# A hybrid attention layer on one core: rope tables in fewer VectorE operations, and a written order from opening to attention

## The chip, the cores and the metric

The kernel runs on one core of one Trainium2 chip. The metric is the device time of one execution in microseconds (us); 0.5% of it is about 5 us. The profile counts from the span's first instruction. PE is TensorE, DVE VectorE, ACT ScalarE, POOL GpSimd, SP the engine whose queue issues nearly all DMAs.

## The reference

One decoder layer over 1024 tokens of width 1024, in float32. The input is normed and modulated (h), one wide projection of h gives the inputs of two attention branches and their gates, each branch is projected back, and the two are merged, projected and added to the input:

```python
h = rmsnorm(x, norm_gain) * (1.0 + scale) + shift
(sb_q, sb_k, sb_v, sb_z, c_q, c_kv, k_rot, mla_z, g_a, g_b) = split(h @ w_in)
o_a = stick_breaking_attention(sb_q, sb_k, sb_v)     # 8 heads of 64
y_a = (o_a * silu(sb_z)) @ w_branch_a
# latent attention: q and k carry 32 rotary columns, rope(x, positions)
y_b = (o_b * silu(mla_z)) @ w_branch_b
x = x + gate * ((sigmoid(g_a) * y_a + sigmoid(g_b) * y_b) @ w_out)
```

`rope` turns 16 pairs of columns by the angles positions * inv_freq. The kernel keeps cos and sin of 1024 tokens x 16 frequencies as two tables of 128 partitions x 128 numbers, which are first used long after, in the latent stage.

## The kernel before

**Split products.** Every operand of a matmul is kept as a rounded part and a remainder (hh and hl, whi and wlo, q0a and so on): a copy into the rounded type (L88 on DVE, L86 on ACT), then a subtraction (`rest`, L96, on DVE or POOL). A product is three matmuls: hi*hi, hi*lo, lo*hi.

**The opening (L419 to L685)** builds hh and hl, eight slices k of h^T, each for two halves q of the tokens, and with them V (four PSUM tiles of tokens) and Q and K of the first head pair (two tiles): `product` L543 adds slice k into six tiles accu[q][0..5] with the PSUM tags g, g, s, s, s, o. The last slice of the second half (L683) goes tile by tile in the order 5, 4, 0, 1, 2, 3, so that ps_o is whole first. For slice k, PE transposes x (L527), ACT writes hh and a full-precision ht (L535), DVE subtracts them into hl (L539, by L96). In the second half the table generator `rope_tables` (L139) is drawn nine yields at a time (L681) between these splits, all on DVE. Its tile rp lies in the buffers of the modulation weights.

**pin_engines (L407)** chains all that was traced since a given point to the previous instruction of the same engine, without semaphores: it fixes each engine's order as written. It is called once, at L685, at the end of the opening. Everything else is ordered by a planner at build time, by its own costs and by when it takes operands to be ready; it also deals out the buffers of a tag. `issue_after(ins)` orders what a block traces on the engine of ins behind ins.

**The change to attention.** Behind L685 stand `evac_q` and `evac_k` (L335, L348) of the first pair: the first half of Q and K was copied to qk0 during the opening, the second lies in accu[1][4] and accu[1][5]. Each half needs 4 ACT copies, 4 DVE remainders and 4 DVE casts, for heads 0 and 1. `store_v` (L565) empties accu[1][0..3]: per tile an ACT copy, a DVE remainder and a DMA to DRAM on SP; `load_v` (L364) reads V of a head pair back. Here the planner chose all orders.

**Jobs (L276).** 30 jobs each project h through 128 columns of w_in: `prep` loads 512 KB of weights on SP (`load_split` L269, into a tile raw of two buffers, a tag shared with qk0), splits them by a cast on DVE (whi) and a subtraction (wlo) on the engine `le`: POOL by default, DVE for job 0. `units` runs 24 matmuls (L299) for each half of the tokens into a PSUM tile by the job's tags; job 0 has tags t and o, most others g and g. `run_jobs` (L304) preps a job between the halves of the one before. The generator is the filler of the attention of head pairs, `sb_pair` (L764), a unit about every second step. A step makes scores on PE (L753), two sigmoids on ACT, a scan on DVE (L757) and a product on POOL (L761); its weights are transposed (L706) and multiplied with V (L723) one step later. Behind L809 jobs 0 and 1 are begun and V of pair 0 is loaded; `gate_sum` (L818) is drawn every fourth step.

Of the kernel before, what the change touches and what calls it, by code (L numbers as in the profile page):

```python
# [19 lines left out]
P = 128  # L20
# [28 lines left out]
def hybrid_layer(ctx: ExitStack, tc: tile.TileContext, x, c, positions, w_ada, b_ada, norm_gain, w_in,  # L49
# [86 lines left out]
    cos_t = base.tile([P, NT, 16], F32, name="cos_t")  # L136
    sin_t = base.tile([P, NT, 16], F32, name="sin_t")

    def rope_tables(pool):  # L139
        eng = nc.vector  # L140
        n = [0]
        slots = pool.tile([P, 32, P], F32, name="rp", tag="wa", bufs=3)

        def new(keep):
            if keep is not None:
                return slots[:, keep]
            n[0] += 1
            return slots[:, n[0] % 26]

        def ts(i, s1, op0, s2=None, op1=None, keep=None):  # L150
            o = new(keep)
            eng.tensor_scalar(out=o, in0=i, scalar1=s1, scalar2=s2, op0=op0, **({"op1": op1} if op1 else {}))
            return o

        def tt(a, b, op, keep=None):
            o = new(keep)
            eng.tensor_tensor(out=o, in0=a, in1=b, op=op)
            return o

        def near(i, unit):  # L160
            m = 1.5 * 2.0 ** 23 * unit
            r = ts(i, m, ALU.add)
            return ts(r, m, ALU.subtract)

        import numpy as np
        inv = np.float32(ROPE_BASE) ** (-np.arange(0, DR, 2, dtype=np.float32) / np.float32(DR))
        ang = new(None)
        av = ang.rearrange("p (t f) -> p t f", f=16)
        for f in range(16):
            eng.tensor_scalar(out=av[:, :, f], in0=pos_c, scalar1=float(inv[f]), scalar2=None,  # L170
                              op0=ALU.mult)
            if f % 4 == 3:
                yield
        from fractions import Fraction
        pi = Fraction(31415926535897932384626433832795028841971693993751, 10 ** 49)
        total = None
        left = ang
        for e in (20, 9, -2, None):
            if e is None:
                part, k, scale = left, Fraction(1) / (2 * pi), 1.0  # L180
            else:
                part = near(left, 2.0 ** e)
                left = tt(left, part, ALU.subtract)
                scale = 2.0 ** -e
                k = Fraction(2) ** e / (2 * pi)
            k -= round(k)
            unit = Fraction(1, 2 ** 12)
            k1 = round(k / unit) * unit
            unit = Fraction(1, 2 ** 24)
            k2 = round((k - k1) / unit) * unit  # L190
            k3 = k - k1 - k2
            whole = ts(part, scale, ALU.mult) if scale != 1.0 else part
            if e is None:
                fr = ts(whole, float(k), ALU.mult)
                total = tt(total, fr, ALU.add)
                break
            t1 = ts(whole, float(k1), ALU.mult)
            yield
            t1 = tt(t1, near(t1, 1.0), ALU.subtract)
            yield  # L200
            t2 = ts(whole, float(k2), ALU.mult)
            yield
            t3 = ts(whole, float(k3), ALU.mult)
            yield
            s = tt(t1, t2, ALU.add)
            yield
            s = tt(s, t3, ALU.add)
            yield
            total = s if total is None else tt(total, s, ALU.add)
            yield  # L210
        turn = tt(total, near(total, 1.0), ALU.subtract)
        yield
        q = ts(near(turn, 0.25), 4.0, ALU.mult, keep=26)
        th = ts(tt(turn, near(turn, 0.25), ALU.subtract), 2.0 * math.pi, ALU.mult, keep=27)
        yield
        t2 = tt(th, th, ALU.mult, keep=28)
        yield

        def poly(cs):
            r = ts(t2, cs[0], ALU.mult, cs[1], ALU.add)  # L220
            for cc in cs[2:]:
                r = ts(tt(r, t2, ALU.mult), cc, ALU.add)
            return r

        fact = math.factorial
        sn = tt(poly([-1.0 / fact(11), 1.0 / fact(9), -1.0 / fact(7), 1.0 / fact(5), -1.0 / fact(3)]), t2, ALU.mult)
        yield
        sn = tt(tt(sn, th, ALU.mult), th, ALU.add, keep=29)
        yield
        cs = tt(poly([1.0 / fact(12), -1.0 / fact(10), 1.0 / fact(8), -1.0 / fact(6), 1.0 / fact(4), -0.5]), t2,  # L230
                ALU.mult)
        cs = ts(cs, 1.0, ALU.add)
        q2 = tt(q, q, ALU.mult)
        yield
        odd = ts(q2, 1.0, ALU.is_equal)
        yield
        m1 = tt(odd, q, ALU.mult)
        yield
        m0 = tt(ts(odd, -1.0, ALU.mult, 1.0, ALU.add), ts(q2, -0.5, ALU.mult, 1.0, ALU.add), ALU.mult)
        yield  # L240
        cv, sv = cos_t.rearrange("p t f -> p (t f)"), sin_t.rearrange("p t f -> p (t f)")
        eng.tensor_tensor(out=cv, in0=tt(m0, cs, ALU.mult), in1=tt(m1, sn, ALU.mult), op=ALU.subtract)
        eng.tensor_tensor(out=sv, in0=tt(m0, sn, ALU.mult), in1=tt(m1, cs, ALU.mult), op=ALU.add)

    def newton(r, v, n):
# [58 lines left out]
    def run_jobs(jobs):  # L304
        for i, j in enumerate(jobs):
            j.prep()
            if i + 1 < len(jobs):
                g = j.units()
                next(g)
                jobs[i + 1].prep()  # L310
                yield
                for _ in g:
                    yield
            else:
                yield from j.units()
# [19 lines left out]
    def evac_q(m):  # L335
        st = pairs[m]

        def f(hf, ps):
            if hf == 0:
                st.q = [qk(f"q{m}a"), qk(f"q{m}b")]  # L340
            s = hsl(hf)
            for h in range(2):
                r0, r1 = (slice(0, 64), slice(64, 128)) if h == 0 else (slice(64, 128), slice(0, 64))
                copy("a", st.q[h][r0, s], ps[r0])
                rest("v", st.q[h][r1, s], ps[r0], st.q[h][r0, s])
        return f

    def evac_k(m):  # L348
        st = pairs[m]

        def f(hf, ps):
            if hf == 0:
                st.k = [qk(f"k{m}a"), qk(f"k{m}b")]
                st.kl = [qk(f"kl{m}a"), qk(f"kl{m}b")]
            s = hsl(hf)
            for h in range(2):
                r0, r1 = (slice(0, 64), slice(64, 128)) if h == 0 else (slice(64, 128), slice(0, 64))
                copy("a", st.k[h][r0, s], ps[r0])
                rest("v", st.kl[h][r0, s], ps[r0], st.k[h][r0, s])
                copy("v", st.k[h][r1, s], rd(st.k[h][r0, s]))  # L360
                copy("v", st.kl[h][r1, s], rd(st.kl[h][r0, s]))
        return f

    def load_v(m):  # L364
        st = pairs[m]
        st.v = sbp.tile([P, NT, 2, P], F32R, name=f"v{m}", tag="v", bufs=2)
        nc.sync.dma_start(out=rd(st.v), in_=v_d[:, :, m])
# [48 lines left out]
    def last_on(name):  # L416
        return last_of[dict(SP=nc.sync, DVE=nc.vector, ACT=nc.scalar, PE=nc.tensor)[name].engine]

    with tc.tile_pool(name="start", bufs=1, **RW, side="right") as st:  # L419
# [145 lines left out]
        def store_v(q, t, pool=st, tag="wa", bufs=3):  # L565
            if pool is st and t % 2 == 0:
                vos[0] = st.tile([P, 2, NPAIR, 2, P], F32R, name="vo", tag="wa", bufs=3)
            vo = vos[0][:, t % 2] if pool is st else pool.tile([P, NPAIR, 2, P], F32R, name="vo", tag=tag, bufs=bufs)
            split_v(vo, accu[q][t], "a")
            nc.sync.dma_start(out=v_d[:, 4 * q + t], in_=rd(vo))  # L570
# [117 lines left out]
    evp = evx.enter_context(tc.tile_pool(name="evp", bufs=2, **RW, side="right"))  # L688
    sbx = ExitStack()
    sbp = sbx.enter_context(tc.tile_pool(name="sbp", bufs=1, **RW, side="right"))  # L690
    for hf in range(2):
        evac_q(0)(hf, qk0[:, 0] if hf == 0 else accu[1][4])
        evac_k(0)(hf, qk0[:, 1] if hf == 0 else accu[1][5])
    for t in range(4):
        store_v(1, t, sbp, "wt", WT_BUFS[0])


    anchor = [None]
    QE = "v"
# [103 lines left out]
    for j, tg in zip(jobs[::-1], "gg,to".split(',')):  # L803
        j.tags = tg
    jobs[0].tags = "to"
    filler = run_jobs(jobs)
    if 1:
        tc.keep_in_program_order(nc.scalar.activation(warm, ones_c, AF.Sigmoid))
    with tc.issue_after(last_on("SP")), tc.issue_after(last_on("DVE")):  # L809
        advance(filler, 1)  # L810
    advance(filler, 1)
    load_v(0)
    ones_r = base.tile([P, 1], F32R, name="ones_r")
    nc.vector.tensor_copy(out=ones_r, in_=ones_c)

# [2 lines left out]
    def gate_sum():  # L818
# [4 lines left out]
            nc.sync.dma_start(out=wgs[k], in_=wada[:, k, 2 * D:3 * D])  # L823

        nc.gpsimd.memset(gsum, 0.0)
        nc.sync.dma_start(out=gsum[0:1], in_=b_ada[:, 2 * D:3 * D])
        load_g(0)
        load_g(1)
        yield
        for k in range(KD):  # L830
            cc = col[:, R_C + k:R_C + k + 1]
# [586 lines left out]
```

## Time and profile before

| | us |
|---|---|
| median of 3 runs | 984.95 (981.52 to 985.64) |
| the profiled execution's own time | 984.33 |
| its span, first to last instruction | 982.5 |
| PE busy | 953.9 (97%) |
| DVE busy | 641.5 (65%) |
| ACT busy | 440.3 (45%) |
| POOL busy | 289.8 (29%) |

Busy shares of PE come from pipelined matmuls, whose ends are modelled: consecutive matmuls overlap in the rows, and the pace is the distance of their starts. In a timeline's row the first number is the start, the second how long the row's instructions lasted together, and the bracket the engine's idle time before them with what ended it. Rows may merge several instructions (x2, x3).

### The profile page before, as it was taken

The numbers are of one execution on the slowest core, as the hardware profiler recorded it, in microseconds if no ns is written. First come the engines' busy times: TensorE is split into PE (matmuls) and PEld (weight loads), VectorE is DVE, ScalarE is ACT, GpSimd is POOL, SyncE is SP. The second block draws the span as 40 slices with busy tenths as digits, with TensorE's granted clock in tenths as the row PEclk, the third lists the DMA queues.
The fourth block names the chain that finished last, engine by engine and source line by source line (L and its number), as shares of the span: only waits on it lengthen the run. The fifth ranks groups of instructions, "written<-read, shape, count | busy, mean of one in ns | idle before, by whom it ended". The sixth has DMA issues, their size and how long they took to land.

```text
span 982.5 us, 14349 instructions
## 1 busy us (share of the span) xinstructions
PE 953.9 (97%) x5132; PEld 824.2 (84%) x5132; DVE 641.5 (65%) x1319; ACT 440.3 (45%) x991; POOL 289.8 (29%) x256
## 2 busy tenths in 40 slices
PE   5999699999999999999999999999999999999997
PEld 4888588888888888888888999988899998878886
DVE  5657756568655966385654454864689997595654
ACT  5453324344524443444443432543488886342211
POOL 1010235344544444354453000621103441101222
PEclk9899899999999999999999999999999999999999
DMA  9911273223331141103212500579554332792232
GB/s 311 332 53 56 87 238 95 73 64 90 129 105 46 54 139 54 54 22 97 76 65 86 150 1 1 192 274 303 180 134 135 104 97 69 248 374 95 83 118 98
DMA packets 112712, 122.39 MB, mean 125 GB/s; under 512 B 14928, under 2 KB 81597, under 8 KB 112256
## 3 DMA queue, kind: packets, MB, share of 16 engines
q1 hardware_dynamic: 112550, 121.44, 39.3%
q8 instruction: 41, 0.67, 0.3%
q14 instruction: 31, 0.25, 0.1%
q10 hardware_dynamic: 90, 0.02, 0.0%
HBM read 86.80 MB, written 34.64 MB: 124 GB/s over the span
## 4 chain that ended last, share of the span: by engine, by line
PE 92%; DVE 4%; DMA 2%; issue 1%; ACT 0%; DVEq 0%; SPq 0%
PE ps_g L299 38%; PE ps_o L723 7%; PE ps_t L706 7%; PE ps_g L935 3%; PE ps_s L1354 3%; PE ps_g L1354 3%; PE ps_t L1354 3%; PE ps_s L936 3%; PE ps_s L1170 2%; PE ps_s L1172 2%; PE ps_s L551 2%; PE ps_s L1171 2%; PE ps_g L551 2%; PE ps_s L754 2%; PE ps_s L753 2%; PE ps_t L1050 2%
## 5 line engine op out<-in xcount | busy, mean ns | idle before, releaser
L299 PE MATMUL ps_g<-hh,whi 128*128 128x512 f32 x448 | 178.8, 399 | 5.4 <-DVE vo L96 5.4
L299 PE MATMUL ps_g<-hl,whi 128*128 128x512 f32 x448 | 177.7, 397 | 0.0
L299 PE MATMUL ps_g<-hh,wlo 128*128 128x512 f32 x448 | 176.8, 395 | 0.0
L757 DVE TENSOR_TENSOR_SCAN surv<-surv,diag 128x128 f32<-128x128 f32 (+3 forms) x64 | 112.6, 1764 | 41.6 <-ACT surv L755 40.8
L96 POOL TENSOR_TENSOR wlo<-raw,whi 128x1024 fp32r<-128x1024 f32 (+1 forms) x37 | 80.8, 2184 | 174.5 <-DVE whi L88 98.2
L96 DVE TENSOR_TENSOR wtl<-ps_t,wth 128x512 fp32r<-128x512 f32 (+1 forms) x192 | 101.6, 548 | 17.6 <-ACT wth L86 16.6
L761 POOL TENSOR_TENSOR beta<-beta,surv 128x127 f32<-128x127 f32 (+3 forms) x64 | 85.4, 1334 | 62.2 <-DVE surv L757 61.6
L299 PEld LDWEIGHTS ps_g<-hh,whi 128*128 128x128 f32 x448 | 85.0, 190 | 21.6 <-DVE vo L96 5.8
L86 ACT ACTIVATE wth<-ps_t 128x512 fp32r<-128x512 f32 (+1 forms) x192 | 90.0, 490 | 23.7 <-PE ps_t L706 21.0
L299 PEld LDWEIGHTS ps_g<-hh,wlo 128*128 128x128 f32 x448 | 84.9, 189 | 17.1
L299 PEld LDWEIGHTS ps_g<-hl,whi 128*128 128x128 f32 x448 | 85.0, 190 | 15.3
L391 ACT ACTIVATE ev<-ps_g 128x512 f32<-128x512 f32 x32 | 19.2, 599 | 105.4 <-PE ps_g L299 103.8
L88 DVE CAST whi<-raw 128x1024 fp32r<-128x1024 f32 (+1 forms) x38 | 24.9, 656 | 57.4 <-PE ps_g L299 43.5
L1182 ACT ACTIVATE sc<-sc,mx 128x128 f32<-128x128 f32 (+3 forms) x64 | 49.3, 771 | 15.0 <-DVE mx L1173 15.0
L1360 POOL TENSOR_TENSOR xr<-xr,fgain 128x512 f32<-128x512 f32 (+1 forms) x17 | 20.9, 1232 | 111.4 <-ACT yr L1359 107.2
L755 ACT ACTIVATE surv<-ps_s 128x512 f32<-128x512 f32 (+2 forms) x96 | 47.1, 494 | 9.0 <-PE ps_s L754 4.4
L756 ACT ACTIVATE beta<-ps_s 128x512 f32<-128x512 f32 (+2 forms) x96 | 47.7, 501 | 3.8 <-POOL beta L761 3.8
L86 ACT ACTIVATE otmp<-ps_o 64x256 f32<-64x256 f32 x64 | 24.2, 379 | 50.0 <-PE ps_o L723 48.9
L706 PE MATMUL ps_t<-ident,sc 128*128 128x128 f32 x288 | 44.9, 275 | 0.1
L706 PE MATMUL ps_t<-ident,beta 128*128 128x128 f32 x288 | 43.1, 275 | 0.0
L299 PE MATMUL ps_g<-oa,whi 128*128 128x512 f32 x128 | 41.3, 397 | 0.0
L1173 DVE CUSTOM_DVE_ANT_0 sc<-ps_s,cmask 128x512 f32<-128x512 f32 (+2 forms) x64 | 37.1, 582 | 5.8 <-PE ps_s L1172 4.4
(420 smaller groups left out, 2350.9 us busy)
## 6 DMA issues: line engine op xcount, KB each, us to landing
raw<-in_w_in SPq DMA_DIRECT2D x35, 512.0 KB, 4.0
wa<-in_w_ada SPq DMA_DIRECT2D x12, 512.0 KB, 6.0
x<-in_x SPq DMA_DIRECT2D x8, 512.0 KB, 5.4
v_d<-vo SPq DMA_DIRECT2D x8, 512.0 KB, 3.4
wg<-in_w_ada SPq DMA_DIRECT2D x8, 512.0 KB, 3.5
ga_d<-ev SPq DMA_DIRECT2D x16, 256.0 KB, 2.0
v<-v_d SPq DMA_DIRECT2D x4, 1024.0 KB
gb_d<-ev SPq DMA_DIRECT2D x16, 256.0 KB, 2.0
```

The source lines that it names most:

```text
L86: nc.scalar.activation(o, i, AF.Copy)
L96: (nc.vector if eng == "v" else nc.gpsimd).tensor_tensor(out=o, in0=full, in1=rd(hi), op=ALU.subtract)
L299: nc.tensor.matmul(out=ps, lhsT=w[:, k, :], rhs=m[k][:, hsl(hf)], start=n == 0, stop=n == last)
L551: nc.tensor.matmul(out=accu[q][unit], lhsT=m[:, tsl], rhs=w[:, 0:512], **fl)
L706: anchor[0] = nc.tensor.transpose(out=pt[:, b * P:(b + 1) * P], in_=w[:, (j0 + b) * P:(j0 + b + 1) * P], identity=ident)
L723: anchor[0] = nc.tensor.matmul(out=po[:, qs], lhsT=vtile(j), rhs=wts[j // 4][n][:, j % 4, qs], start=j == 0 and n == 0, stop=j == i and n ...
L755: nc.scalar.activation(surv[:, c0:c0 + wc], ps[:, 0:wc], AF.Sigmoid, scale=-0.125)
L756: nc.scalar.activation(beta[:, c0:c0 + wc], ps[:, 0:wc], AF.Sigmoid, scale=0.125)
L757: scan[0] = nc.vector.tensor_tensor_scan(out=surv[:, 0:w][:, ::-1], data0=surv[:, 0:w][:, ::-1], data1=diag1[:, S - w:S][:, ::-1], initial ...
L761: nc.gpsimd.tensor_tensor(out=beta[:, 0:w - 1], in0=beta[:, 0:w - 1], in1=surv[:, 1:w], op=ALU.mult)
L1182: nc.scalar.activation(sc[:, 0:w], sc[:, 0:w], AF.Exp, bias=mx[:, len(chunks) - 1:len(chunks)] if CH else mx[:, 0:1], scale=-1.0, accum_ou ...
L1354: nc.tensor.matmul(out=ps[:, 0:wc], lhsT=m[k][:, tsl], rhs=w[:, k, cs], start=k == 0 and i == 0, stop=k == KD - 1 and i == 2)
```

## The change

The table generator computes the same tables with other operations: a tile inv_t, filled by 16 memsets on POOL, makes the angles in one operation; `near` adds and subtracts its constant in one; products and sums are joined into scalar_tensor_tensor. The emptying of Q, K and V, the preparation of jobs 0 and 1 and the load of V are traced in one written sequence and pinned. Job 1's wlo goes to DVE. The second halves of Q and K are emptied head by head, with the Sigmoid warm-up between them. The start of gate_sum's DMAs is put behind V's load on SP.

```diff
@@ -136,6 +136,12 @@
     cos_t = base.tile([P, NT, 16], F32, name="cos_t")
     sin_t = base.tile([P, NT, 16], F32, name="sin_t")
 
+    import numpy as np
+    inv = np.float32(ROPE_BASE) ** (-np.arange(0, DR, 2, dtype=np.float32) / np.float32(DR))
+    inv_t = base.tile([P, 16], F32, name="inv_t")
+    for f in range(16):
+        nc.gpsimd.memset(inv_t[:, f:f + 1], float(inv[f]))
+
     def rope_tables(pool):
         eng = nc.vector
         n = [0]
@@ -157,20 +163,20 @@
             eng.tensor_tensor(out=o, in0=a, in1=b, op=op)
             return o
 
+        def stt(a, c, b, op0, op1, keep=None):
+            o = new(keep)
+            eng.scalar_tensor_tensor(out=o, in0=a, scalar=c, in1=b, op0=op0, op1=op1)
+            return o
+
         def near(i, unit):
             m = 1.5 * 2.0 ** 23 * unit
-            r = ts(i, m, ALU.add)
-            return ts(r, m, ALU.subtract)
-
-        import numpy as np
-        inv = np.float32(ROPE_BASE) ** (-np.arange(0, DR, 2, dtype=np.float32) / np.float32(DR))
+            return ts(i, m, ALU.add, m, ALU.subtract)
+
         ang = new(None)
-        av = ang.rearrange("p (t f) -> p t f", f=16)
-        for f in range(16):
-            eng.tensor_scalar(out=av[:, :, f], in0=pos_c, scalar1=float(inv[f]), scalar2=None,
-                              op0=ALU.mult)
-            if f % 4 == 3:
-                yield
+        eng.tensor_tensor(out=ang.rearrange("p (t f) -> p t f", f=16),
+                          in0=pos_c[:, :, None].broadcast_to([P, NT, 16]),
+                          in1=inv_t[:, None, :].broadcast_to([P, NT, 16]), op=ALU.mult)
+        yield
         from fractions import Fraction
         pi = Fraction(31415926535897932384626433832795028841971693993751, 10 ** 49)
         total = None
@@ -189,57 +195,53 @@
             unit = Fraction(1, 2 ** 24)
             k2 = round((k - k1) / unit) * unit
             k3 = k - k1 - k2
-            whole = ts(part, scale, ALU.mult) if scale != 1.0 else part
             if e is None:
-                fr = ts(whole, float(k), ALU.mult)
-                total = tt(total, fr, ALU.add)
+                total = stt(part, float(k), total, ALU.mult, ALU.add)
                 break
-            t1 = ts(whole, float(k1), ALU.mult)
+            t1 = ts(part, scale, ALU.mult, float(k1), ALU.mult)
             yield
             t1 = tt(t1, near(t1, 1.0), ALU.subtract)
             yield
-            t2 = ts(whole, float(k2), ALU.mult)
+            s = stt(part, scale * float(k2), t1, ALU.mult, ALU.add)
             yield
-            t3 = ts(whole, float(k3), ALU.mult)
-            yield
-            s = tt(t1, t2, ALU.add)
-            yield
-            s = tt(s, t3, ALU.add)
+            s = stt(part, scale * float(k3), s, ALU.mult, ALU.add)
             yield
             total = s if total is None else tt(total, s, ALU.add)
             yield
         turn = tt(total, near(total, 1.0), ALU.subtract)
         yield
-        q = ts(near(turn, 0.25), 4.0, ALU.mult, keep=26)
-        th = ts(tt(turn, near(turn, 0.25), ALU.subtract), 2.0 * math.pi, ALU.mult, keep=27)
+        quarter = near(turn, 0.25)
+        q = ts(quarter, 4.0, ALU.mult, keep=26)
+        yield
+        th = ts(tt(turn, quarter, ALU.subtract), 2.0 * math.pi, ALU.mult, keep=27)
         yield
         t2 = tt(th, th, ALU.mult, keep=28)
         yield
 
-        def poly(cs):
-            r = ts(t2, cs[0], ALU.mult, cs[1], ALU.add)
-            for cc in cs[2:]:
-                r = ts(tt(r, t2, ALU.mult), cc, ALU.add)
+        def poly_t2(cs):
+            r = ts(t2, cs[0], ALU.mult)
+            for cc in cs[1:]:
+                r = stt(r, cc, t2, ALU.add, ALU.mult)
             return r
 
         fact = math.factorial
-        sn = tt(poly([-1.0 / fact(11), 1.0 / fact(9), -1.0 / fact(7), 1.0 / fact(5), -1.0 / fact(3)]), t2, ALU.mult)
+        sn = poly_t2([-1.0 / fact(11), 1.0 / fact(9), -1.0 / fact(7), 1.0 / fact(5), -1.0 / fact(3)])
         yield
         sn = tt(tt(sn, th, ALU.mult), th, ALU.add, keep=29)
         yield
-        cs = tt(poly([1.0 / fact(12), -1.0 / fact(10), 1.0 / fact(8), -1.0 / fact(6), 1.0 / fact(4), -0.5]), t2,
-                ALU.mult)
+        cs = poly_t2([1.0 / fact(12), -1.0 / fact(10), 1.0 / fact(8), -1.0 / fact(6), 1.0 / fact(4), -0.5])
+        yield
         cs = ts(cs, 1.0, ALU.add)
         q2 = tt(q, q, ALU.mult)
         yield
         odd = ts(q2, 1.0, ALU.is_equal)
-        yield
         m1 = tt(odd, q, ALU.mult)
         yield
-        m0 = tt(ts(odd, -1.0, ALU.mult, 1.0, ALU.add), ts(q2, -0.5, ALU.mult, 1.0, ALU.add), ALU.mult)
+        m0 = stt(odd, 1.0, ts(q2, 0.5, ALU.mult, 1.0, ALU.subtract), ALU.subtract, ALU.mult)
         yield
         cv, sv = cos_t.rearrange("p t f -> p (t f)"), sin_t.rearrange("p t f -> p (t f)")
         eng.tensor_tensor(out=cv, in0=tt(m0, cs, ALU.mult), in1=tt(m1, sn, ALU.mult), op=ALU.subtract)
+        yield
         eng.tensor_tensor(out=sv, in0=tt(m0, sn, ALU.mult), in1=tt(m1, cs, ALU.mult), op=ALU.add)
 
     def newton(r, v, n):
@@ -335,11 +337,11 @@
     def evac_q(m):
         st = pairs[m]
 
-        def f(hf, ps):
-            if hf == 0:
+        def f(hf, ps, heads=(0, 1)):
+            if hf == 0 and 0 in heads:
                 st.q = [qk(f"q{m}a"), qk(f"q{m}b")]
             s = hsl(hf)
-            for h in range(2):
+            for h in heads:
                 r0, r1 = (slice(0, 64), slice(64, 128)) if h == 0 else (slice(64, 128), slice(0, 64))
                 copy("a", st.q[h][r0, s], ps[r0])
                 rest("v", st.q[h][r1, s], ps[r0], st.q[h][r0, s])
@@ -348,12 +350,12 @@
     def evac_k(m):
         st = pairs[m]
 
-        def f(hf, ps):
-            if hf == 0:
+        def f(hf, ps, heads=(0, 1)):
+            if hf == 0 and 0 in heads:
                 st.k = [qk(f"k{m}a"), qk(f"k{m}b")]
                 st.kl = [qk(f"kl{m}a"), qk(f"kl{m}b")]
             s = hsl(hf)
-            for h in range(2):
+            for h in heads:
                 r0, r1 = (slice(0, 64), slice(64, 128)) if h == 0 else (slice(64, 128), slice(0, 64))
                 copy("a", st.k[h][r0, s], ps[r0])
                 rest("v", st.kl[h][r0, s], ps[r0], st.k[h][r0, s])
@@ -688,12 +690,6 @@
     evp = evx.enter_context(tc.tile_pool(name="evp", bufs=2, **RW, side="right"))
     sbx = ExitStack()
     sbp = sbx.enter_context(tc.tile_pool(name="sbp", bufs=1, **RW, side="right"))
-    for hf in range(2):
-        evac_q(0)(hf, qk0[:, 0] if hf == 0 else accu[1][4])
-        evac_k(0)(hf, qk0[:, 1] if hf == 0 else accu[1][5])
-    for t in range(4):
-        store_v(1, t, sbp, "wt", WT_BUFS[0])
-
 
     anchor = [None]
     QE = "v"
@@ -803,13 +799,25 @@
     for j, tg in zip(jobs[::-1], "gg,to".split(',')):
         j.tags = tg
     jobs[0].tags = "to"
+    jobs[0].le = jobs[1].le = "v"
     filler = run_jobs(jobs)
-    if 1:
-        tc.keep_in_program_order(nc.scalar.activation(warm, ones_c, AF.Sigmoid))
-    with tc.issue_after(last_on("SP")), tc.issue_after(last_on("DVE")):
+    first = len(traced)
+    jobs[0].prep()
+    evac_q(0)(0, qk0[:, 0])
+    evac_k(0)(0, qk0[:, 1])
+    jobs[1].prep()
+    for t in range(4):
+        store_v(1, t, sbp, "wt", WT_BUFS[0])
+    for h in range(2):
+        evac_q(0)(1, accu[1][4], (h,))
+        evac_k(0)(1, accu[1][5], (h,))
+        if h == 0:
+            nc.scalar.activation(warm, ones_c, AF.Sigmoid)
+    load_v(0)
+    pin_engines(first)
+    with tc.issue_after(last_on("ACT")), tc.issue_after(last_on("DVE")):
         advance(filler, 1)
     advance(filler, 1)
-    load_v(0)
     ones_r = base.tile([P, 1], F32R, name="ones_r")
     nc.vector.tensor_copy(out=ones_r, in_=ones_c)
 
@@ -823,9 +831,10 @@
             nc.sync.dma_start(out=wgs[k], in_=wada[:, k, 2 * D:3 * D])
 
         nc.gpsimd.memset(gsum, 0.0)
-        nc.sync.dma_start(out=gsum[0:1], in_=b_ada[:, 2 * D:3 * D])
-        load_g(0)
-        load_g(1)
+        with tc.issue_after(last_on("SP")):
+            nc.sync.dma_start(out=gsum[0:1], in_=b_ada[:, 2 * D:3 * D])
+            load_g(0)
+            load_g(1)
         yield
         for k in range(KD):
             cc = col[:, R_C + k:R_C + k + 1]
```

## Rows read from the trace of the kernel before

**Rows 1.** What PE waited for: us in total, times, longest.

```profile
PE ps_g L299 <- DVE vo L96: 5.4, 1, 5.4
...
PE ps_o L554 <- DVE hl L96: 2.3, 1, 2.3
```

**Rows 2.** Timeline of PE, 106 to 128 us.

```profile
106.10 0.50 PE L554 MATMUL ps_o<-hl,w3h 128*128 128x512 f32 x1 [2.26 <-DVE hl L96]
...
107.14 0.63 PE L551 MATMUL ps_g<-w3h,hh 128*128 128x512 f32 x1
...
110.55 0.40 PE L551 MATMUL ps_s<-w3h,hl 128*128 128x512 f32 x1
...
116.74 0.39 PE L299 MATMUL ps_t<-hh,wlo 128*128 128x512 f32 x1
122.50 0.80 PE L299 MATMUL ps_g<-hh,whi 128*128 128x512 f32 x1 [5.37 <-DVE vo L96]
...
127.70 0.39 PE L299 MATMUL ps_g<-hh,whi 128*128 128x512 f32 x1
```

**Rows 3.** Windows: length; busy of PE, PEld, DVE, ACT, POOL; clock, DMA, GB/s.

```profile
122.40:128.00 5.60, 5.50 (x14) 4.37 (x15) 5.35 (x11) 0.11 (x1) 0.00 (x0) 0.54 0.86 331
...
130.00:548.00 418.00, 417.55 (x2172) 354.96 (x2171) 261.44 (x308) 173.48 (x393) 190.68 (x190) 1.00 0.28 85
548.00:982.50 434.50, 426.11 (x2461) 378.09 (x2460) 295.30 (x783) 211.39 (x512) 85.75 (x53) 1.00 0.46 147
```

**Rows 4.** Timeline of DVE, 88 to 124 us.

```profile
88.71 0.69 DVE L96 TENSOR_TENSOR hl<-ht,hh 128x512 fp32r<-128x512 f32 x1 [0.62 <-ACT ht L535]
...
95.50 0.68 DVE L96 TENSOR_TENSOR hl<-ht,hh 128x512 fp32r<-128x512 f32 x1
...
105.36 0.68 DVE L96 TENSOR_TENSOR hl<-ht,hh 128x512 fp32r<-128x512 f32 x1
...
106.75 1.23 DVE L96 TENSOR_TENSOR wlo<-raw,whi 128x1024 fp32r<-128x1024 f32 x1
113.37 0.69 DVE L88 CAST whi<-raw 128x1024 fp32r<-128x1024 f32 x1 [5.39 <-DMA raw<-in_w_in]
...
114.81 2.77 DVE L96 TENSOR_TENSOR q0b<-qk,q0b 64x512 fp32r<-64x512 f32 x1
...
123.67 0.42 DVE L88 CAST kl0a<-kl0a 64x512 fp32r<-64x512 f32 x1
```

**Rows 5.** Timeline of ACT, 97 to 115 us.

```profile
97.13 0.77 ACT L535 ACTIVATE ht<-ps_t,ab 128x512 f32<-128x512 f32 x1
...
113.04 1.28 ACT L808 ACT_TABLE_LOAD   x1
```

**Rows 6.** The table's tile rp: duration ns min/median/max, first and last start us, forms.

```profile
L152 DVE TENSOR_SCALAR rp<-rp x46: 219/226/229, 81.4 to 103.3; 128x128 f32<-128x128 f32 x46
L157 DVE TENSOR_TENSOR rp<-rp x36: 283/293/295, 81.9 to 104.8; 128x128 f32<-128x128 f32 x36
L170 DVE TENSOR_SCALAR rp<-pos_c x16: 166/168/170, 80.1 to 81.2; 128x8 f32<-128x8 f32 x16
```

**Rows 7.** Groups of DVE instructions by shape: busy us, mean ns.

```profile
L497 DVE SCALAR_TENSOR_TENSOR acc<-wa,col,acc 128x512 f32<-128x512 f32 x15 | 11.2, 748 | 0.3
...
L497 DVE SCALAR_TENSOR_TENSOR acc<-wa,col,acc 128x256 f32<-128x256 f32 x9 | 4.4, 484 | 0.3
```

**Rows 8.** Timeline of POOL, two stretches.

```profile
9.23 3.32 POOL L483 TENSOR_SCALAR x<-x,r 128x1024 f32<-128x1024 f32 x1 [7.95 <-ACT jk L464]
...
114.20 2.84 POOL L96 TENSOR_TENSOR wlo<-raw,whi 128x1024 fp32r<-128x1024 f32 x1 [61.67 <-DVE whi L88]
```

**Rows 9.** Timeline of SP's queue, 40 to 175 us.

```profile
131.81 1.33 SPq L367 DMA_DIRECT2D v<-v_d  x2
```

**Rows 10.** The page's DMA issues: KB each, median us from issue to landing.

```profile
v_d<-vo SPq DMA_DIRECT2D x8, 512.0 KB, 3.4
```

**Rows 11.** The page's costliest groups: busy us, mean ns of one.

```profile
L757 DVE TENSOR_TENSOR_SCAN surv<-surv,diag 128x128 f32<-128x128 f32 (+3 forms) x64 | 112.6, 1764 | 41.6 <-ACT surv L755 40.8
```

## The prediction

> **What bounds the kernel now.** I read the list of what TensorE (PE) waited for first. Two of its entries lie in the stretch that the change touches: 5.4 us before a ps_g tile that VectorE (DVE) still had to empty, and 2.3 us before a slice of hl, also DVE's [rows 1]. PE's own timeline places them: the matmul at 106.10 stood 2.26 us behind its predecessor, the one at 122.50 stood 5.37 [rows 2]. The windows say what follows a pause and how full PE is elsewhere: the granted clock was 0.54 in 122.4 to 128, near the lower of its two levels (1.2 GHz against 2.4); from 130 to 548 PE was busy for 417.55 of 418 us, from there on for 426.11 of 434.5 [rows 3]. So PE is the bound, little behind 130 waits, and time taken out of 103 to 128 should reach the end. The DVE timeline shows whose delay it is: hl's last split ran at 105.36, after the whole table, though ScalarE (ACT) had its input ready from 97.13 + 0.77 = 97.9 on; then whi of job 1 stood 5.39 us waiting for its load, while q, k and V, which needed no load, were queued behind it [rows 4, 5].
>
> **What the two pauses cost.** At full clock matmuls start 6.19 / 27 = 0.229 us apart (110.55 to 116.74, 27 starts later). From 107.14 to 110.55 there are 8 starts, 3.41 us where 8 x 0.229 = 1.83 would do: 1.58 lost. From 122.50 to 127.70 there are 12, 5.20 us for 2.75: 2.45 lost [rows 2]. With the idle times: 2.26 + 1.58 + 5.37 + 2.45 = 11.7 us. That is the most that these two places can give back.
>
> **The table.** The old generator issues 100 DVE operations: 46 with one tensor (L152), 38 with two (36 at L157, then L242 and L243), 16 narrow ones (L170). The new one, counted through its loops, issues 57: 18 with one tensor, 22 with two, 17 scalar_tensor_tensor. The first three cost 226, 290 and 168 ns [rows 6]. A scalar_tensor_tensor of 128 columns isn't in the trace; L497 took 484 ns at 256 columns and 748 at 512 [rows 7], 1.03 ns a column, so 352 at 128 is my estimate. Its bounds are 290 (a two-tensor operation of its width) and 484. The old sum is 10.4 + 11.0 + 2.7 = 24.1 us; on the clock the table took from 80.10 to 105.36, 25.3 us, less three splits of hl at 0.69 and about 0.8 of waiting: 22.4, since independent neighbours overlap. The new sum is 4.07 + 6.38 + 5.98 = 16.4, times 22.4 / 24.1 gives 15.3; at the bounds 14.3 and 17.4. Half as many operations are a third of the time.
>
> More than the sum, its place matters. Nine yields per k are drawn as before, but they now hold 14, 15, 25 and 3 operations, and each split of hl stands between two such blocks: 3.6, 3.9, 7.0 and 0.8 us. From 80.1 and with 0.69 for each split, hl[6] ends near 97 (its old split stood at 95.5, and PE did not wait for it) and hl[7] could start at 97.5; its input comes at 97.9, so it ends at 98.6. At the upper bound, with no overlap at all, the sum is 18.7 and hl[7] ends at 101.6. PE wants it at 106.10 - 2.26 = 103.84. The first pause goes at either bound. The 16 new memsets of one column stand at the start of POOL, which waited 7.95 us for its first large operation [rows 8]: nothing, unless together they took that long.
>
> **The order after it.** DVE now runs, in a written order: whi and wlo of job 0; eight operations on the first half of q and k; whi and wlo of job 1; four remainders of V; eight operations on the second half. Prices: 0.69 for whi, 1.23 for wlo, 0.69 for a remainder, 0.42 for a cast [rows 4].
> - Job 0's weights end at 98.6 + 0.69 + 1.23 = 100.5. Before, they followed hl's split without a wait, so their load is early enough.
> - First half of q and k: 4 x 0.69 + 4 x 0.42 = 4.4, to 105.0. It reads qk0, which ACT, free from 97.9, copies meanwhile.
> - Job 1's load takes the buffer that job 0's raw weights leave at 100.5 and needs about the 5.4 us that DVE waited for it before: 105.9. This is the one wait on a load in DVE's new order; queued behind it are all of V and the second halves. The other buffer of that tag is qk0's, free only at 104.1; if the load gets that one, everything from here is 3.6 us later.
> - whi and wlo of job 1 end at 107.8, V's remainders at 108.5 to 110.6, the last remainder that ps_o needs (k of head 1) at 114.2, the last cast at 115.
>
> PE, unbroken from 103.84, ends the opening's 16 remaining matmuls at 107.5 and job 0's first half, 24 matmuls, at 113.0. It then wants ps_g (free at 108.5, in the later case 112.1) and job 1's weights (107.8 or 111.4). Both are there, with 4.5 us to spare or 0.9; at the table's upper bound, 3 us later, 1.5. So the second pause goes too, and without pauses I expect no stretch at the lower clock.
>
> Job 1's wlo moves from POOL (2.84 us) to DVE (1.23). **A rule weighed here:** beside that POOL operation, at 114.20, DVE's q0b remainder took 2.77 us, against 0.69 for others of its kind [rows 4, 8]. The Trainium skill (GPSIMD Engine Reference, Key points) says that POOL shares its SBUF interfaces with VectorE, with contention where VectorE runs a two-port mode or reads two SBUF inputs. The trace agrees in this row. By that rule moving wlo helps, yet POOL's two memsets and a cast (diag1, gsum), which have no written place, may now slow the pinned operations. By the row alone, 0 to 2.1 us; I take 0 for the sum, as 2.1 lies inside PE's 4.5 us of cover, and keep 2.1 for the range.
>
> ACT's order now has the Sigmoid table load, 1.28 us [rows 5], between the second halves of heads 0 and 1; behind it stand q and k of head 1. With 0.69 for a copy, ACT makes one of V and two more behind PE's 107.5, then the load, then two: 112.3, before DVE wants the last one at 113.5. Nothing. On SP the load of V, issued at 131.81 before [rows 9], now stands directly behind V's four stores; one landed in 3.4 us [rows 10], so SP stands until about 114. Behind it come gsum, wg and perhaps job 2's weights. Job 2's whi can't be written before job 0's second half leaves its tile, 118.5 if that runs next and 124 if as before, and job 1 is still to run then: a load of 5.4 us from 114 on is covered. Nothing again. The written order is silent on PE: the jobs' matmuls lie outside it and are placed by the planner.
>
> **Sum.** 11.7 us off the profiled execution's 984.33 gives 972.6; that execution lies 0.6 under the median of 984.95, so I forecast 973.2. Its own range is 971 to 975.5: the 11.7 holds within some 1.5 (one stretch at the lower clock kept), and the shown runs differ by 4.
>
> **Rivals.**
> - **ps_o second.** The planner may put job 0's second half (ps_o) directly behind its first. PE then waits from 113.0 to 114.2, and a short pause cost 1.58 of clock before: 2.8 lost, 976.0. For it: it is next in program order. Against: V is emptied first, so ps_g is free sooner, and before the planner took the tile that came free first.
> - **The same, with the load in qk0's buffer.** ps_o is free at 117.8: 4.8 idle and 2.45 of clock, 7.3 lost, 980.5; with POOL's 2.1 it is 982.6. Against: before, the load went as soon as job 0's raw was split, so buffers are given as they come free.
> - **A new order for the rest (slower).** Only this stretch is written down; attention is placed by the planner again. There each of 64 steps needs a scan of 1.76 us on DVE [rows 11] between a sigmoid and the transposes on PE, so far hidden under the jobs' matmuls. Each one exposed costs PE at least that: with seven the gain is spent, with ten the kernel ends near 991. Place: 130 to 548. Against: 0.45 us of idle there before [rows 3], and the same jobs remain to fill with.
> - **The change does less than it says:** the planner could have had this order already. On DVE it had not [rows 4], and DVE is what PE waited for.
>
> **Chances.** Forecast 0.61, ps_o second 0.17, with the late load 0.10, a new order 0.12. Faster by over 0.5% means under 980.0, slower means over 989.9; that is about what a measurement of this kernel can tell from no change. The forecast and the first rival are faster, 0.78, and 0.02 of a new order that costs little: 0.80. The late load and another 0.04 are within 0.5%: 0.14. Slower: 0.06. Range 970.5 to 980.5: below, all of the 11.7 and part of the spread of the runs; above, ps_o second with POOL's 2.1 and that spread. The late load with POOL, and most of a new order, lie outside.
>
> **What would show it.** Right: no idle time of PE before the opening's ps_o matmul, hl's last split at about 98, granted clock 1.0 through 103 to 128, V's remainders ending near 111, V loaded before 120, and PE behind that point as full as before. Table wrong: DVE between 80 and 101 still filled, a scalar_tensor_tensor near 484 ns. Order wrong: DVE idle over 3 us before job 1's whi, PE idle near 113 before ps_o or ps_g. Wrong as a whole: PE is some 10 us ahead at 130, and the end does not move.

## The result, and the profile after

The changed kernel took 970.62 us (median of 4 runs, 968.70 to 971.47) against 985.30 (4 runs, 981.52 to 985.82): a ratio of 0.9858, 95% interval 0.984 to 0.9877. A second set of 4 runs gave 972.74 (969.42 to 974.34), so all eight have a median of 971.4. The forecast was 973.2 in a range of 970.5 to 980.5: the first median lies just inside the range's lower end and under the 971 that the prediction gives for the forecast's own spread, the median of all eight inside both. The profiled execution took 969.88 us, with a span of 968.1.

The list of what PE waited for, of the changed kernel (us in total, times, longest). Both entries of [rows 1] are gone:

```profile
PE ps_t L122 <- DMA vec<-in_norm_gain: 5.9, 1, 5.9
PE ps_t L508 <- DMA wa<-in_w_ada: 4.0, 2, 3.8
PE ps_t L512 <- DVE acc L499: 1.6, 1, 1.6
PE ps_g L301 <- ACT whi L86: 1.5, 1, 1.5
```

PE's timeline, answering to [rows 2]: the first matmul that needs hl's last split, the first of job 0, the first of job 1, the first of job 0's second half. None has a bracket, so none stood idle; job 1 follows job 0 at the same 0.23 us as everything else.

```profile
101.39 0.39 PE L556 MATMUL ps_o<-hl,w3h 128*128 128x512 f32 x1
...
105.02 0.39 PE L301 MATMUL ps_t<-hh,whi 128*128 128x512 f32 x1
...
110.23 0.39 PE L301 MATMUL ps_t<-hh,wlo 128*128 128x512 f32 x1
110.46 0.39 PE L301 MATMUL ps_g<-hh,whi 128*128 128x512 f32 x1
...
117.40 0.39 PE L301 MATMUL ps_o<-hh,whi 128*128 128x512 f32 x1
```

Windows of the changed kernel (columns as in [rows 3]): the stretch of the change, attention, and the stages behind it.

```profile
103.00:130.00 27.00, 27.00 (x128) 22.58 (x127) 14.69 (x24) 11.61 (x25) 6.09 (x8) 1.00 0.81 268
...
125.00:537.00 412.00, 411.55 (x2148) 350.40 (x2147) 258.45 (x303) 171.25 (x384) 187.42 (x184) 1.00 0.28 82
544.00:968.00 424.00, 414.73 (x2397) 366.71 (x2395) 292.36 (x778) 207.69 (x505) 85.83 (x53) 1.00 0.46 146
```

The same 27 us of the kernel before are one row:

```profile
103.00:130.00 27.00, 19.37 (x67) 14.95 (x66) 20.27 (x35) 7.14 (x12) 5.15 (x4) 0.81 0.51 168
```

128 matmuls in place of 67, at a granted clock of 1.00 in place of 0.81. Behind it PE idles as little as in [rows 3]: 0.45 us in attention, 9.3 in the rest (8.4 before), and not at all in the 7 us between the two windows. So the time came out of this stretch, and of idle time no more than 0.9 us was given back later.

DVE's timeline, answering to [rows 4]: the fourth split of hl, the table's first operation, hl[6], hl[7], job 1's whi, and V's four remainders. Then the table's tile rp by kind (ns minimum/median/maximum), answering to [rows 6]:

```profile
77.50 0.69 DVE L96 TENSOR_TENSOR hl<-ht,hh 128x512 fp32r<-128x512 f32 x1 [1.13 <-ACT ht L537]
78.11 0.28 DVE L176 TENSOR_TENSOR rp<-pos_c,inv_t 128x128 f32<-128x128 f32 x1
...
90.68 1.60 DVE L168 SCALAR_TENSOR_TENSOR rp<-rp 128x128 f32<-128x128 f32 x5
...
94.56 0.68 DVE L96 TENSOR_TENSOR hl<-ht,hh 128x512 fp32r<-128x512 f32 x1
...
95.89 0.69 DVE L96 TENSOR_TENSOR hl<-ht,hh 128x512 fp32r<-128x512 f32 x1
...
103.00 0.69 DVE L88 CAST whi<-raw 128x1024 fp32r<-128x1024 f32 x1
...
104.94 1.37 DVE L96 TENSOR_TENSOR vo<-ps_g,vo 128x512 fp32r<-128x512 f32 x2
106.23 1.28 DVE L96 TENSOR_TENSOR vo<-ps_s,vo 128x512 fp32r<-128x512 f32 x2
```

```profile
L163 DVE TENSOR_TENSOR rp<-rp x19: 283/292/293, 78.7 to 95.4; 128x128 f32<-128x128 f32 x19
L158 DVE TENSOR_SCALAR rp<-rp x18: 219/226/230, 78.4 to 93.2; 128x128 f32<-128x128 f32 x18
L168 DVE SCALAR_TENSOR_TENSOR rp<-rp x17: 285/292/295, 79.7 to 93.5; 128x128 f32<-128x128 f32 x17
```

hl[7] ends at 96.58, 4.8 us before PE wants it. Job 1's whi has no bracket: its load was there. V's first remainder ends near 105.6, also 4.8 us before PE wants ps_g at 110.46.

**A yardstick for single profiles.** Two executions of one kernel can differ by some 3 us for a reason that lies ahead of the change. The fourth split of hl in the second half, the last DVE work before the table, starts at 79.49 in the kernel before (the row below) and 77.50 in the changed one, but at 80.74 and 80.37 when both were profiled again. So 2.0 of the 14.4 us between the first two spans are no gain of the change. From here on a profile is measured from that split to the end of the span:

```profile
79.49 0.69 DVE L96 TENSOR_TENSOR hl<-ht,hh 128x512 fp32r<-128x512 f32 x1 [1.14 <-ACT ht L535]
```

| kernel | 4th split | to PE's first matmul of job 1 | from there to the end | split to end |
|---|---|---|---|---|
| before | 79.49 | 43.0 | 860.0 | 903.0 |
| e0, before again | 80.74 | 42.6 | 860.0 | 902.6 |
| changed | 77.50 | 33.0 | 857.6 | 890.6 |
| e7, changed again | 80.37 | 33.0 | 859.2 | 892.1 |
| e1, table only | 80.70 | 34.2 | 858.3 | 892.5 |
| e2, order only | 78.00 | 36.3 | 857.6 | 893.9 |
| e3, wlo of job 1 on POOL | 80.66 | 33.0 | 859.2 | 892.1 |
| e4, no written order | 82.11 | 33.0 | 856.6 | 889.6 |
| e5, 6 products more | 80.67 | 33.0 | 857.3 | 890.2 |
| e6, 16 products more | 80.36 | 35.6 | 856.8 | 892.4 |

### The profile page after: what moved, and what is told of

Its sections match the earlier page's. It is cut to its first block, busy times and chain, and to the rows that moved or that the text cites. A ratio compares the mean times of both kernels' runs of the same rounds, so it can differ in the third digit from the quotient of the medians.

```text
span 968.1 us, 14331 instructions
## 1 busy us (share of the span) xinstructions
PE 945.7 (98%) x5132; PEld 818.4 (85%) x5132; DVE 633.2 (65%) x1277; ACT 440.2 (45%) x991; POOL 287.8 (30%) x271
## 4 chain that ended last, share of the span: by engine, by line
PE 93%; DMA 4%; DVE 1%; ACT 0%; issue 0%; SPq 0%; POOL 0%; DVEq 0%; ACTq 0%; POOLq 0%
PE ps_g L301 37%; PE ps_o L719 7%; PE ps_t L702 7%; PE ps_g L944 3%; PE ps_g L1363 3%; PE ps_s L1363 3%; PE ps_t L1363 3%; PE ps_s L945 3%; PE ps_g L553 3%; PE ps_s L553 2%; PE ps_s L1179 2%; PE ps_s L1181 2%; PE ps_s L1180 2%; PE ps_s L750 2%; PE ps_s L749 2%; PE ps_t L1059 2%
## 5 line engine op out<-in xcount | busy, mean ns | idle before, releaser
L753 DVE TENSOR_TENSOR_SCAN surv<-surv,diag 128x128 f32<-128x128 f32 (+3 forms) x64 | 109.6, 1717 | 47.6 <-ACT surv L751 46.5
L96 POOL TENSOR_TENSOR wlo<-raw,whi 128x1024 fp32r<-128x1024 f32 (+1 forms) x36 | 78.0, 2166 | 113.9 <-DVE whi L88 36.3
L756 POOL MEMSET beta<- 128x1 f32 x64 | 6.7, 104 | 128.0 <-ACT beta L752 125.0
L731 POOL TENSOR_TENSOR oga<-oga,zs 64x256 f32<-64x256 f32 x32 | 36.0, 1126 | 20.2 <-DVE oga L729 19.0
```

What stands on the lines that cost most here:

```text
L96: (nc.vector if eng == "v" else nc.gpsimd).tensor_tensor(out=o, in0=full, in1=rd(hi), op=ALU.subtract)
L753: scan[0] = nc.vector.tensor_tensor_scan(out=surv[:, 0:w][:, ::-1], data0=surv[:, 0:w][:, ::-1], data1=diag1[:, S - w:S][:, ::-1], initial ...
```

## The experiments

**e0 and e7: both kernels again**, unchanged.

> The kernel before, unchanged, for a second profile. Theory (the 2 us by which the changed kernel was ahead before the table began is the phase in which the clock rises in an execution): ratio 1.000 within 0.003; the pauses of 2.3 and 5.4 us before ps_o and ps_g stand again, but the time at which hl[3] of the second half is split, 79.5 in one profile, may differ by 1 to 2 us from it. Rival (the 2 us belong to the change): hl[3] at 79.5 within 0.3 us here.

> The changed kernel once more, for a second profile. Theory: the part of the opening that no part of the change touches (the fourth split of hl, 77.5 us in its first profile against 79.5 and 80.7 in two of the kernel before) varies with the execution by 2 to 3 us and is no gain of the change; from there to the end some 890.6 us again, within 1 us, and no pause before ps_o or ps_g. Rival (the change makes the opening faster as well): the fourth split again at 77 to 78 us.

e0: 985.02 us (10 runs), ratio 0.9999 (0.9981 to 1.0018). Its two pauses were 2.3 and 5.0 us. e7: 972.74, ratio 0.988 (0.984 to 0.992), no pause in the stretch. The fourth split came at 80.37, so the rival that the change makes the opening faster falls. The part to job 1 is 33.0 again; the 1.6 us that e7 has more behind it lie in one place, where PE waited 1.9 us for a whi of the last branch:

```profile
865.65 1.62 PE L301 MATMUL ps_g<-ob,whi 128*128 128x512 f32 x4 [1.88 <-ACT whi L86]
```

The window 860 to 880 of e7 then shows a granted clock of 0.91, so the lower level for part of it; in the changed kernel's first profile it is 1.00 after a wait of 1.53 in the same place (window of e7, then wait and window of the first profile):

```profile
860.00:880.00 20.00, 18.12 (x73) 14.49 (x72) 14.90 (x24) 6.53 (x11) 0.00 (x0) 0.91 0.82 291
```

```profile
862.69 1.19 PE L301 MATMUL ps_g<-ob,whi 128*128 128x512 f32 x4 [1.53 <-ACT whi L86]
```

```profile
860.00:880.00 20.00, 18.47 (x82) 14.77 (x81) 14.51 (x23) 6.06 (x10) 0.00 (x0) 1.00 0.69 242
```

**e1: the new table alone**, in the kernel before.

```diff
-    (rope_tables, near, inv of the kernel before)
+    (inv_t and rope_tables of the changed kernel)
```

> The kernel before with the new table generator alone, job orders as before. Theory (two pauses, each with its own cause, second one set by DVE's order): the first pause goes, 2.3 + 1.6 us; DVE is 7 us earlier at job 0's weights, but still stands some 5 us before job 1's whi with q, k and V behind it, so V's first remainder ends 9 us after that load, near 115, and PE, 4 us earlier at 113, waits some 2 us for ps_g and loses 1.6 of clock: in all 8 us faster, ratio 0.992. Rival (the table is all that matters): no pause before ps_g, 11.7 us, 0.988. Rival (order is all): 3.8 us, 0.996.

972.26 us, ratio 0.9875 (0.9852 to 0.9897). The first pause is gone, the second shrinks to 1.08 us. DVE still stands before job 1's weights, and the work it then does first still goes ahead of V (DVE, then POOL, then PE):

```profile
99.09 0.69 DVE L96 TENSOR_TENSOR hl<-ht,hh 128x512 fp32r<-128x512 f32 x1
...
105.76 0.69 DVE L88 CAST whi<-raw 128x1024 fp32r<-128x1024 f32 x1 [4.05 <-DMA raw<-in_w_in]
...
107.20 2.78 DVE L96 TENSOR_TENSOR q0b<-qk,q0b 64x512 fp32r<-64x512 f32 x1
...
114.15 1.29 DVE L96 TENSOR_TENSOR vo<-ps_g,vo 128x512 fp32r<-128x512 f32 x2
```

```profile
106.59 2.84 POOL L96 TENSOR_TENSOR wlo<-raw,whi 128x1024 fp32r<-128x1024 f32 x1 [53.79 <-DVE whi L88]
```

```profile
114.89 0.50 PE L301 MATMUL ps_g<-hh,whi 128*128 128x512 f32 x1 [1.08 <-DVE vo L96]
```

**e2: the written order alone**, with the old table. Job 1's wlo on DVE, the emptying head by head and the order on SP are in it, as in the changed kernel.

```diff
-    (evac_q, evac_k, store_v at the opening's end; warm; load_v behind the filler)
+    first = len(traced)
+    jobs[0].prep()
...
+    load_v(0)
+    pin_engines(first)
```

> The changed kernel with the old table generator: only the written order. Theory: the first pause stays, 2.3 us and 1.6 of clock; hl[7] ends at 106, V's first remainder some 10 us later at 116, PE wants ps_g at 117: no second pause, 7.8 us faster, ratio 0.992. Rival (table is all that matters): V is late by the table's 7 us, PE waits 3 us or more for ps_g: under 5 us faster, 0.995 or more. Rival (order is all): 11.7 us, 0.988.

974.14 us, ratio 0.9896 (0.9873 to 0.9919). The first pause stays as it was, the second is 0.24:

```profile
104.61 0.50 PE L554 MATMUL ps_o<-hl,w3h 128*128 128x512 f32 x1 [2.26 <-DVE hl L96]
...
114.33 0.50 PE L299 MATMUL ps_g<-hh,whi 128*128 128x512 f32 x1 [0.24 <-DVE vo L96]
```

Neither part was worth the 8 us that I had expected of it; each gave most of the whole. The reason is that the second pause is a difference of two times. Counted from the fourth split, e1's job 1 weights are cast at 105.76 - 80.70 = 25.1 us, in the kernel before at 113.37 - 79.49 = 33.9 [rows 4]: DVE's chain to V comes 8.8 us earlier, of which the table is 7.5 (hl[7] starts at 99.09 - 80.70 = 18.4 against 105.36 - 79.49 = 25.9) and the shorter wait for the load, 4.05 against 5.39, the rest. PE, without the first pause, wants ps_g at 113.81 - 80.70 = 33.1 against 117.13 - 79.49 = 37.6, so 4.5 earlier. That leaves 5.37 - 8.8 + 4.5 = 1.1 of the second pause, and 1.08 was measured. The sums close: table alone, with a granted clock of 1.00 behind the pause of 1.08 us, 2.26 + 1.58 + (5.37 - 1.08) + 2.45 = 10.6, measured 903.0 - 892.5 = 10.5. Order alone keeps the 2.26 but not the slow clock behind it: 1.58 + (5.37 - 0.24) + 2.45 = 9.2, measured 9.1.

That clock is the surprise. The same pause of 2.26 us was followed by the lower level in the kernel before and in e0 (2.25 there), and not in e2. The 5.9 us behind it, of e0 and of e2:

```profile
107.40:113.30 5.90, 5.90 (x19) 4.70 (x20) 1.71 (x2) 2.29 (x5) 0.00 (x0) 0.71 0.52 156
```

```profile
104.60:110.50 5.90, 5.89 (x25) 4.82 (x26) 5.61 (x9) 2.68 (x6) 0.00 (x0) 1.00 0.33 89
```

**e3: job 1's wlo left on POOL**, all else as changed.

```diff
-    jobs[0].le = jobs[1].le = "v"
+    jobs[0].le = "v"
```

> The changed kernel with job 1's wlo on POOL again. Theory (V's remainders had 4.8 us to spare, and DVE is spared 1.23 us): DVE operations beside POOL's 2.8 us get up to 2.1 us longer, V ends within 1 us of where it did, no pause of PE: same time as the changed kernel, ratio to the kernel before 0.986 within 0.002. Rival (the move of wlo was a needed part): PE pauses before ps_g, for wlo or for V, ratio 0.989 or more.

971.88 us, ratio 0.9868 (0.9845 to 0.9891); no pause, 33.0 us to job 1 as in the changed kernel. Beside POOL's operation here stand remainders of V at their usual price, not one of q at 2.8:

```profile
106.97 2.41 POOL L96 TENSOR_TENSOR wlo<-raw,whi 128x1024 fp32r<-128x1024 f32 x1 [40.84 <-DVE whi L88]
```

```profile
106.96 0.69 DVE L96 TENSOR_TENSOR vo<-ps_g,vo 128x512 fp32r<-128x512 f32 x1
108.78 0.69 DVE L96 TENSOR_TENSOR vo<-ps_g,vo 128x512 fp32r<-128x512 f32 x1 [1.12 <-ACT vo L86]
```

The 859.2 from job 1 on are e7's too, and for the same reason: PE waited 1.59 us for the late whi, and the window 860 to 880 has a granted clock of 0.91. The move to DVE gained nothing that can be measured.

**e4: the same tracing without the written order.**

```diff
     load_v(0)
-    pin_engines(first)
```

> The changed kernel without the written order of the stretch: the new table stays, and so does the new sequence in which the stretch is traced, but the planner orders every engine. Theory (the table shortens the way to hl[7], and the written order only has to keep job 1's weights from standing ahead of V): the planner again puts work that PE does not want first ahead of V's four remainders, as it did in the kernel before, but DVE is ahead by the table's 7 us; so at most a pause like the 1.1 us of the run with the new table alone, no half-clock stretch, 971 to 974 us. Rival (the written order carries most of the gain): a pause of over 3 us before ps_g or ps_o, some 977 to 980 us.

973.82 us, ratio 0.9897 (0.9857 to 0.9938), and no pause in the stretch. The planner did what the theory hadn't thought of. Job 0's weights and job 1's whi go ahead of hl[7], which comes 105.32 - 82.11 = 23.2 us after the fourth split (18.4 in the changed kernel), and PE runs job 0's matmuls inside the opening (the fourth split, then PE):

```profile
82.11 0.69 DVE L96 TENSOR_TENSOR hl<-ht,hh 128x512 fp32r<-128x512 f32 x1 [1.14 <-ACT ht L537]
```

```profile
103.95 0.39 PE L556 MATMUL ps_o<-hh,w3l 128*128 128x512 f32 x1
104.18 0.39 PE L301 MATMUL ps_t<-hh,whi 128*128 128x512 f32 x1
...
107.81 0.39 PE L301 MATMUL ps_t<-hl,whi 128*128 128x512 f32 x1
108.03 0.61 PE L553 MATMUL ps_g<-w3h,hl 128*128 128x512 f32 x2
```

Work was exchanged, not lost: job 1 starts 33.0 us after the split, as in the changed kernel, and to the end it is 889.6 against 890.6 and 892.1. So the rival that the pinning carries the gain falls; beside the new table, the planner's own order is as good behind the split, and nearly so in e1, whose tracing is the old one. The median lies above the changed kernel's by 1 to 3 us, with an interval that holds both. In e4's profile the excess stands ahead of the split, which is the latest of all; PE waited 3.5 us there for acc, a wait of 1.6 in the changed kernel's list above. Whether that is e4's plan or scatter, one profile doesn't tell. The emptying head by head, the place of the Sigmoid load and the order on SP were not tried by themselves.

**e5 and e6: DVE work added** between cos and sin, ahead of hl[7]; its results are not used.

```diff
         eng.tensor_tensor(out=cv, ...)
         yield
+        for _ in range(6):      # e6: 16
+            eng.tensor_tensor(out=slots[:, 30:32], in0=slots[:, 26:28], in1=slots[:, 28:30], op=ALU.mult)
```

> The changed kernel with 6 DVE products of 128x256 more in the table, between cos and sin and so ahead of hl's last split; their results are not used. At 0.42 to 0.45 us each (290 ns at 128 columns, 484 at 256 for the two nearest kinds) that is 2.6 us. Theory (after the change DVE is off the path here, with slack of its own): hl[7] ends some 2.6 us later, at 99.2 on the clock of the changed kernel's profile, PE wants it at about 101.4, V's remainders end at 110 against 110.5 for ps_g: no pause over 0.5 us, and the time within 1.5 us of the changed kernel's. Rival (every us of DVE work ahead of V still costs a us): 973 us.

> The same with 16 products more, some 6.9 us. Theory: hl[7] ends near 103.5 on that clock against 101.4, so PE stands about 2 us before ps_o; V's remainders end near 114.4, and PE, now 2 us later, wants ps_g at 112.5: another 2 us. In all 4 us of pauses, 3 to 6 us more than the changed kernel with what the clock takes, 974 to 977. If the time lies within 1 us of the changed kernel's, the slack is larger than the rows say, and the two pauses of the kernel before had another cause than DVE's lateness.

e5: 972.40 us, ratio 0.9877 (0.9842 to 0.9912). The six took 2.7 us and cost nothing: 890.2 to the end, no pause. e6: 974.58, ratio 0.9893 (0.9849 to 0.9938). Sixteen took 7.3 us, and the first pause is back (DVE, then PE):

```profile
98.02 7.32 DVE L246 TENSOR_TENSOR rp<-rp 128x256 f32<-128x256 f32 x16
...
105.99 0.68 DVE L96 TENSOR_TENSOR hl<-ht,hh 128x512 fp32r<-128x512 f32 x1
...
115.22 1.28 DVE L96 TENSOR_TENSOR vo<-ps_g,vo 128x512 fp32r<-128x512 f32 x2
```

```profile
106.72 0.50 PE L558 MATMUL ps_o<-hl,w3h 128*128 128x512 f32 x1 [2.31 <-DVE hl L96]
...
115.96 0.50 PE L303 MATMUL ps_g<-hh,whi 128*128 128x512 f32 x1
```

hl[7] came 105.99 - 98.76 = 7.2 us later than in e7 (which has the same fourth split; its hl[7] is the first row below), and 2.3 of these showed: the slack is 4.9 us. Of my 4 us of pauses only the first came. I had counted all four remainders of V for the second, but ps_g is free behind the first one, which ends near 115.9, just in time for 115.96. The granted clock after this pause was 1.00, so 2.31 is its whole price; 892.4 against 890.2 in e5 is 2.2 (the window is the second row below):

```profile
98.76 0.69 DVE L96 TENSOR_TENSOR hl<-ht,hh 128x512 fp32r<-128x512 f32 x1
```

```profile
106.70:112.60 5.90, 5.88 (x26) 4.88 (x27) 5.61 (x9) 2.75 (x6) 0.00 (x0) 1.00 0.35 91
```

## Why the prediction was right

**The bound and the two pauses.** Right. From the fourth split to job 1 the kernel before needs 43.0 us, the changed one 33.0: 10.0 for the 2.26 + 1.58 + 5.37 = 9.2 that stood there. The prediction called its 11.7 the most that the two places can give back, and that was a little low: a bracket counts from a matmul's modelled end, 0.39 us after its start, though the next one could start after 0.23. From 116.74 to 122.50 [rows 2] 5.76 - 0.23 = 5.53 us were lost, not 5.37, and as much more at the first pause; the other 0.5 are spread over the stretch. From job 1 on it is 860.0 against 857.6: 2.4 for the 2.45 of clock. Together 12.4 for a forecast 11.7; e7, with its late stretch at the lower clock, gives 10.9. The eight runs lie 13.6 below the median of 985.0 that e0's runs show, 1 to 3 more than these profiles account for. Where that sits, no run shows; the intervals are about as wide. Of the 2.6 us by which the first median lies under the forecast, the profiles explain 0.7 (12.4 for 11.7); for the rest no cause is shown.

**The table.** The mechanism and the counts were right, the price of a scalar_tensor_tensor was not. I took 352 ns, by 1.03 ns a column from L497, between bounds of 290 and 484. It took 292, the lower bound: what a product of two tensors costs. The slope a column was right, but the row that I drew it from stands higher throughout: L497's 484 and 748 are 59 and 58 ns above a product of two tensors of 256 columns (425 in e6's added products) and a split of hl at 512 (690), and 352 is 60 above 292. L497 takes its scalar from a tile (col), the table's are constants; that this makes the 60 ns no run shows by itself. Five in a row took 1.60 us, 0.32 each. The sum is then 4.07 + 22 x 0.29 + 17 x 0.292 = 15.4 instead of 16.4. On the clock the table runs from 78.11 to 95.98: 17.9 us, less three splits of hl at 0.69 and 0.2 of waiting, 15.6. That is 1.01 of the sum, where I had carried over the old table's 22.4 / 24.1 = 0.93. So two terms were off, in opposite directions, and that 15.6 stands beside a forecast 15.3 is luck. "Half as many operations are a third of the time" was loosely said: 57 operations in place of 100 took 15.6 us in place of 22.4, about a third less. hl[7] ended 19.1 us after the fourth split began (96.58 - 77.50), as forecast: 98.6 - 79.49 = 19.1.

**The order.** Right in its outcome: 4.8 us to spare at ps_g, forecast 4.5. One term was too dear. I let job 1's load take 5.4 us, so that DVE would stand before whi; the buffer was free at 98.5 and whi ran at 103.00 without a wait, so it took at most 4.5. In e1 the same load took 4.05 behind wlo's end, in e2 5.2. V's first remainder ended 105.6 - 77.5 = 28.1 us after the fourth split began, where 108.5 - 79.5 = 29.0 was forecast. The load took the buffer of job 0's raw weights, not qk0's: that rival did not occur.

**ps_o second.** Did not occur: job 1's first half came before job 0's second, as at 110.46 and 117.40 above. **A new order for the rest.** Attention was planned anew and lost nothing, 0.45 us idle as before. **POOL.** The two memsets and the cast that I feared beside the pinned operations ran far earlier, the last at 62.02, and POOL stood still until 116.32. The 16 memsets of one column took 0.7 us at its start, inside a wait of 7.8. In e1 q0b beside POOL's wlo took 2.78 us again; e3's remainders of V beside the same operation took 0.69. The Trainium skill (GPSIMD Engine Reference, Key points) says that POOL shares its SBUF interfaces with VectorE, with contention where a VectorE instruction runs a two-port mode or reads two SBUF inputs. Both rows agree: q0b reads two SBUF tiles, V's remainders PSUM and one SBUF tile. This was not tried further.

**SP.** V's load did not go as one behind the stores: half went at 114.43, the other at 118.69, with gsum, ga_d and wg between. PE first takes V at 128.4, and nothing waited for it:

```profile
105.66 4.19 SPq L572 DMA_DIRECT2D v_d<-vo  x4
114.43 0.62 SPq L369 DMA_DIRECT2D v<-v_d  x1
...
118.69 0.54 SPq L369 DMA_DIRECT2D v<-v_d  x1
```

**What the steps could not see.** I priced the two parts as one and nothing in the forecast depended on it, but the split that I expected afterwards, 8 us each, was wrong: once either is in place, the other adds 1.9 us (order) or 3.3 (table) by the first profile, and 1.5 us less than that by e7's, which has the lower clock late in the kernel.

## What to carry to other kernels

A pause before a full PE is a difference between two chains: what each cure is worth must be worked out with the other cure in place, since here either of two changes alone brought about three quarters or more of what both bring together. Once such a place has slack, say how much (4.8 us here): six more products cost nothing, and sixteen cost only what lay beyond it. Before comparing two single profiles, find a point ahead of the change and measure from there, or the start's own scatter (3 us here) is read as a gain.

## What had not been expected of the hardware

The clock that a pause costs is not fixed. Pauses of 2.26 and 2.25 us were followed by a stretch at the lower level in two profiles of the kernel before (0.71 over 5.9 us in e0), which cost 1.58 us in the first; pauses of 2.26 in e2 and 2.31 in e6 were followed by a clock of 1.00. Late in the kernel, at one and the same wait for a whi, 1.88 us in e7 and 1.59 in e3 were followed by 0.91 over 20 us, 1.53 in the changed kernel's first profile, 1.59 in e0 and 1.71 in e4 by 1.00. So the length of the pause alone does not decide it, and what does these runs don't tell. A forecast should give that term as a range from nothing up, not as a fixed addition.
